# Sliding-window attention in zero-padded blocks of 128 keys, and carried memories' rows loaded straight into 128-row tiles

## The chip, the cores and the metric

One Trainium2 chip, one of its cores. A core has five engines with instruction queues of their own: TensorE (PE in the profile, with its weight loads as PEld), VectorE (DVE), ScalarE (ACT), GpSimd (POOL) and SyncE (SP, which here only starts DMAs). The metric is the device time of one launch in microseconds (us), the median of several runs.

## The reference

Two layers of a trunk, applied to a prompt of 512 tokens without history and to 8 samples of 16 tokens with carried state; width 1024, all in fp32. Per layer:

```
u = rms_norm(x);  z = u @ w_in                       # 1024 -> 10504 columns, split into 14 pieces
y_a = (rg_lru(conv(xa)) * gelu(ga)) @ w_oa           # linear recurrence
y_b = (rms_norm(mlstm(q,k,v,gates)) * sigmoid(mo)) @ w_ob     # 4 heads of 256, matrix memories C
y_c = banded_attention(q,k,v, window 128, sinks) @ w_oc       # 16 heads of 64, 2 key/value heads
x += (sigmoid(g_a)*y_a + sigmoid(g_b)*y_b + sigmoid(g_c)*y_c) @ w_out
x += square(relu(rms_norm(x) @ w_up)) @ w_down       # 1024 -> 4096 -> 1024
```

Attention works on chunks of 64 queries. A chunk sees the 128 keys before it and its own 64, so 192 keys; the first two chunks of the prompt see 64 and 128. A sample's 16 queries see 128 cached keys and 16 new ones. Scores get a softmax with an extra sink term in the denominator, `p = exp(s-mx) / (sum + exp(sink-mx))`, and then `p @ v`. For the samples the mLSTM also updates each carried memory, `C_new = decay*C + sum_s wk_s k_s v_s^T`, for 8 samples x 4 heads.

## The kernel before

Tokens are 640 columns (512 of the prompt, 128 of the samples). Every large projection is `gemm_w` (line 154: weights stationary, 320 token columns a matmul, issued on line 167) or `gemm_x` (line 173: tokens stationary, 256 weight columns, line 185). For accuracy a weight block is split into a rounded part (ACT, line 142) and a remainder (DVE, line 143), and both are multiplied in fp32r, which the trace shows as one instruction a matmul; a plain fp32 matmul is two, a transpose (a matmul against the identity) one.

The program is written with a scheduler that fixes each engine's order at build time from its own cost estimates. So attention and mLSTM matmuls stand among those of projections, and an engine runs its list strictly in order. What follows is the code around the change.

Attention (`attention`, from line 603). For each of 8 pairs of query heads, `prompt_pair` (line 694) goes through four groups G of two 64-query chunks. A group has one PSUM bank from `ps_small` (four such banks). Scores (line 705) are [128 = two heads x 64 queries, up to 192 keys] a chunk; `softmax` (line 679) takes the maximum, the exponentials, the sums and the division; the result P is transposed in two pieces, 128 keys (line 714) and 64 keys (line 717); both are copied to SBUF (pT), and line 740 multiplies them with the values: a matmul whose contraction has 128 rows and one with 64. Odd chunks need values that are shifted by 64 rows, which the copy vB holds. `sample_group` (line 748) does the same for one key/value head's 8 samples, two at a time, with 128 cached keys (line 786) and 16 new ones (line 787, contraction of 16 rows). It runs twice a layer, after the second and the fourth block of query heads; after the second run attention is over.

mLSTM (`mlstm`, from line 402). For each head, `sample` (line 425) writes the split keys and values of the samples to a DRAM scratch (sdr) and reads them back by groups of two samples: `rows(g)` loads 48 rows (16 of each of three products) into a staging tile `kvr`, of which there are two, DVE copies that into the fp32r tile `kvs` (line 441), of which there is one, and line 461 multiplies with a contraction of 48 rows. Line 457 reads the memory with the queries, line 463 adds the product to it.

Of the kernel before, what the change touches and what calls it, by code (L numbers as in the profile page):

```python
# [60 lines left out]
def trunk(ctx: ExitStack, tc: tile.TileContext, I, O):  # L61
# [3 lines left out]
    pe, act, dve, pool, sp = nc.tensor, nc.scalar, nc.vector, nc.gpsimd, nc.sync  # L65
# [11 lines left out]
    ident = cs[:, 0:128]  # L77
# [16 lines left out]
    def ps_small():  # L94
        return psB.tile([128, 512], F32, name="psb", tag="psb")
# [184 lines left out]
    with tc.tile_pool(name="ld", bufs=1) as ld:  # L280
# [121 lines left out]
    def mlstm(l, gp, gpp, mp, half, hdp):  # L402
# [200 lines left out]
    def attention(l, ap):  # L603
# [16 lines left out]
        def norm_rope(q, n, tabs, out):  # L620
# [6 lines left out]
            dve.tensor_tensor(t1, q, q, ALU.mult)  # L627
# [49 lines left out]

        def softmax(units, sink, P):

            n = len(units)  # L680
            sm = ap.tile([128, 20], F32, name="ssm", tag="ssm", bufs=3)
            mx, nm, sums, es, rc = [sm[:, 4 * i:4 * i + n] for i in range(5)]
            for i, (s, k) in enumerate(units):
                dve.tensor_reduce(mx[:, i:i + 1], s, AX.X, ALU.max)
            dve.tensor_scalar(nm, mx, sink, -1.0, op0=ALU.max, op1=ALU.mult)  # L685
            for i, (s, k) in enumerate(units):
                act.activation(P[:, i, 0:k], s, AF.Exp, bias=nm[:, i:i + 1], accum_out=sums[:, i:i + 1])  # L687
# [3 lines left out]
            for i, (s, k) in enumerate(units):  # L691
                dve.tensor_scalar(P[:, i, 0:k], P[:, i, 0:k], rc[:, i:i + 1], None, op0=ALU.mult)

        def prompt_pair(pair, g, q):
            yo = ap.tile([128, 512], F32, name="yo", tag="yo", bufs=2)
            for G in range(4):
                units = []
                ps = ps_small()
                for cc in range(2):
                    c = 2 * G + cc  # L700
                    k0 = max(0, 64 * (c - 2))
                    k = 64 * (c + 1) - k0
                    s = ps[:, 256 * cc:256 * cc + 192]
                    for part in range(2):
                        pe.matmul(s, q[:, c].rearrange("p a d -> p (a d)"), kh[g][:, part, k0:k0 + 192],  # L705
                                  start=(part == 0), stop=(part == 1))
                    units.append((s[:, 0:k], k))
                P = ap.tile([128, 2, 192], F32, name="P", tag="P", bufs=4)
                softmax(units, sinkp[:, pair:pair + 1], P)
                pT = ap.tile([128, 4, 128], F32, name="pT", tag="pT", bufs=2)  # L710
                for cc in range(2):
                    c = 2 * G + cc
                    if c > 0:
                        pe.transpose(ps[:, 128 * cc:128 * cc + 128], P[:, cc, 0:128], ident)  # L714
                    if c != 1:
                        o = 0 if c == 0 else 128
                        pe.transpose(ps[0:64, 256 + 128 * cc:384 + 128 * cc], P[:, cc, o:o + 64], ident)
                pv = ps.rearrange("p (a b) -> p a b", a=4)
                if G == 0:
                    act.copy(pT[:, 1, :], pv[:, 1, :])  # L720
                    dve.tensor_copy(pT[0:64, 2, :], pv[0:64, 2, :])
                else:
                    act.copy(pT[:, 0:2, :], pv[:, 0:2, :])
                    dve.tensor_copy(pT[0:64, 2:4, :], pv[0:64, 2:4, :])
                for cc in range(2):
                    c = 2 * G + cc
                    o = ps[:, 128 * cc:128 * cc + 128]

                    def vv_(t_, j, n):
                        return t_[0:n, j, g].rearrange("p a d -> p (a d)")  # L730
                    if c == 1:
                        parts = [(vv_(vd, 0, 128), pT[:, 1, :])]
                    elif c == 0:
                        parts = [(vv_(vd, 0, 64), pT[0:64, 2, :])]
                    elif c % 2 == 0:
                        parts = [(vv_(vd, (c - 2) // 2, 128), pT[:, 0, :]), (vv_(vd, c // 2, 64), pT[0:64, 2, :])]
                    else:
                        parts = [(vv_(vB, (c - 3) // 2, 128), pT[:, 1, :]), (vv_(vB, (c - 1) // 2, 64), pT[0:64, 3, :])]
                    for n, (a, b) in enumerate(parts):
                        pe.matmul(o, a, b, start=(n == 0), stop=(n == len(parts) - 1))  # L740
                pov = ps[:, 0:256].rearrange("p (c r q) -> p c r q", c=2, r=2)
                for r in range(2):
                    sl = slice(64 * r, 64 * r + 64)
                    eng = act.copy if r else dve.tensor_copy
                    eng(yo[sl, 128 * G:128 * G + 128].rearrange("p (c q) -> p c q", c=2), pov[sl, :, r, :])  # L745
            sp.dma_start(ydr[1][128 * pair:128 * pair + 128, 0:512], yo)

        def sample_group(g):
            vn = ap.tile([16, 8, 2, 64], F32, name="vn", tag="t2")
            for b in range(DB):  # L750
                sp.dma_start(vn[:, b], vd[16 * b:16 * b + 16, 4, g])
# [12 lines left out]
            act.copy(kcT[:, :, 128:144], ks[g].rearrange("p (b s) -> p b s", s=16))  # L764
            yo = ap.tile([128, 4, 128], F32, name="yo", tag="yo", bufs=2)
            for b2 in range(4):
                units = []
                ps = ps_small()
                for bb in range(2):
                    s = ps[:, 256 * bb:256 * bb + 144]  # L770
                    b = 2 * b2 + bb
                    pe.matmul(s, qsm[:, b].rearrange("p a q -> p (a q)"), kcT[:, b, :], start=True, stop=True)
                    units.append((s, 144))
                P = ap.tile([128, 2, 192], F32, name="P", tag="P", bufs=4)
                softmax(units, sinks[:, g:g + 1], P)
                pT = ap.tile([128, 4, 128], F32, name="pT", tag="pT", bufs=2)
                for bb in range(2):
                    pe.transpose(ps[:, 128 * bb:128 * bb + 128], P[:, bb, 0:128], ident)
                    pe.transpose(ps[0:16, 256 + 128 * bb:384 + 128 * bb], P[:, bb, 128:144], ident)
                pv = ps.rearrange("p (a b) -> p a b", a=4)  # L780
                act.copy(pT[:, 0:2, :], pv[:, 0:2, :])
                dve.tensor_copy(pT[0:16, 2:4, :], pv[0:16, 2:4, :])
                for bb in range(2):
                    b = 2 * b2 + bb
                    o = ps[:, 128 * bb:128 * bb + 128]
                    pe.matmul(o, vc[:, b].rearrange("p a d -> p (a d)"), pT[:, bb, :], start=True, stop=False)  # L786
                    pe.matmul(o, vn[:, b].rearrange("p a d -> p (a d)"), pT[0:16, 2 + bb, :], start=False, stop=True)  # L787
                pov = ps[:, 0:256].rearrange("p (b i r q) -> p b i r q", b=2, i=4, r=2)
                for r in range(2):
                    sl = slice(64 * r, 64 * r + 64)  # L790
                    eng = act.copy if r else dve.tensor_copy
                    eng(yo[sl, :, 32 * b2:32 * b2 + 32].rearrange("p i (b q) -> p b i q", b=2), pov[sl, :, :, r, :])
# [422 lines left out]
```

## Time and profile before

| | us |
|---|---|
| median of 3 runs (lowest to highest) | 3022.73 (3021.82 to 3025.65) |
| the profiled execution | 3022.11 |
| its span, first to last instruction | 3020.3 |
| PE busy | 2980.8 (99%) |
| DVE busy | 1594.3 (53%) |
| ACT busy | 1162.2 (38%) |
| POOL busy | 295.5 (10%) |

Matmuls are pipelined: the one that follows starts while the one before drains, so the mean duration of a group of matmuls is longer than what it adds to the time. What one adds is the distance between the starts, or the ends, of neighbours. Times in the timeline count from the span's start; the first layer ends at about 1520 us, the second repeats it. Attention's first scores stand at 250 us and its last products at 514 us, mLSTM's samples between 590 and 880 us.

### The profile page before, as it was taken

Reading aid. Unit: us, or ns where it says so; the run is one execution under the profiler, and the core shown is the slowest. Engines: PE = TensorE matmul, PEld = TensorE weight load, DVE = VectorE, ACT = ScalarE, POOL = GpSimd, SP = SyncE. Lnnn points to the kernel's source line nnn. Section 1 sums busy time; section 2 is a strip of 40 time slices with the busy share of each in tenths; the row PEclk is TensorE's granted clock in tenths of the full one; section 3 lists DMA queues with packets and bytes.
Section 4 is the critical chain, followed back from the end, with each engine's and each line's share of the span. In section 5 each row is a group of like instructions: output and inputs, shape, how many; then the busy total and the mean of one; then the engine's idle time right before and its main releaser. Section 6 shows DMA issues by size and latency. Waiting matters only on the chain.

```text
span 3020.3 us, 51634 instructions
## 1 busy us (share of the span) xinstructions
PE 2980.8 (99%) x20742; PEld 2894.7 (96%) x20742; DVE 1594.3 (53%) x3460; ACT 1162.2 (38%) x2409; POOL 295.5 (10%) x357
## 2 busy tenths in 40 slices
PE   8999999999999999999999999999999999999999
PEld 8999998999999999999999999989999999999999
DVE  7967565445564443333479666554455544433332
ACT  5754443433432332232348443433333323322322
POOL 0300000111102010010012000001010120100100
PEclk9999998999999999999999999989999999999999
DMA  5232221444565322222322322224444743222222
GB/s 167 71 110 76 66 89 58 133 131 139 152 214 180 105 70 84 71 72 83 101 85 66 114 81 66 90 73 132 133 145 147 243 123 111 70 76 79 70 79 76
DMA packets 291216, 319.59 MB, mean 106 GB/s; under 512 B 26424, under 2 KB 259688, under 8 KB 290944
## 3 DMA queue, kind: packets, MB, share of 16 engines
q1 hardware_dynamic: 281440, 300.03, 32.6%
q10 hardware_dynamic: 9536, 16.26, 1.5%
q8 instruction: 163, 2.67, 0.4%
q14 instruction: 77, 0.63, 0.1%
HBM read 255.76 MB, written 62.04 MB: 105 GB/s over the span
## 4 chain that ended last, share of the span: by engine, by line
PE 92%; DVE 3%; DMA 2%; ACT 2%; issue 1%; SPq 0%; POOL 0%; ACTq 0%; DVEq 0%; POOLq 0%
PE acc L167 62%; PE acc L185 17%; PE psb L740 3%; PE psb L461 1%; PE psb L705 1%; PE psb L457 1%; PE psb L550 1%; PE psb L997 1%; DVE wlo L143 1%; PE psb L546 1%; PE psb L787 1%; PE psb L536 1%; PE psb L543 1%; PE psb L786 0%; PE psb L714 0%
## 5 line engine op out<-in xcount | busy, mean ns | idle before, releaser
L167 PE MATMUL acc<-at,whi 128*128 128x320 f32 x8960 | 1394.4, 311 | 4.2 <-DVE sg L904 2.4
L167 PEld LDWEIGHTS acc<-at,whi 128*128 128x128 f32 x8960 | 1331.8, 188 | 11.5 <-DVE sg L904 3.0
L167 PE MATMUL acc<-at,wlo 128*128 128x320 f32 x4480 | 721.4, 310 | 0.0
L167 PEld LDWEIGHTS acc<-at,wlo 128*128 128x128 f32 x4480 | 670.0, 188 | 3.4
L142 ACT CAST whi<-wraw 128x512 fp32r<-128x512 f32 (+1 forms) x712 | 428.5, 619 | 596.1 <-PE acc L167 524.5
L143 DVE TENSOR_TENSOR wlo<-wraw,whi 128x512 fp32r<-128x512 f32 (+1 forms) x712 | 474.1, 704 | 294.7 <-ACT whi L142 191.7
L185 PE MATMUL acc<-whi,at 128*128 128x256 f32 (+1 forms) x3040 | 411.9, 286 | 10.1 <-DVE sg L864 3.0
L185 PEld LDWEIGHTS acc<-whi,at 128*128 128x128 f32 x3040 | 380.6, 190 | 15.7 <-ACT vt L497 3.9
L185 PE MATMUL acc<-wlo,at 128*128 128x256 f32 (+1 forms) x1520 | 219.1, 284 | 0.0
L185 PEld LDWEIGHTS acc<-wlo,at 128*128 128x128 f32 x1520 | 196.7, 190 | 1.3
L1136 POOL TENSOR_TENSOR ha<-ha 128x640 f32<-128x640 f32 x64 | 82.2, 1284 | 824.3 <-DVE ha L1135 824.3
L1144 DVE TENSOR_TENSOR x<-x,acc 128x640 f32<-128x640 f32 x56 | 45.8, 818 | 153.4 <-PE acc L167 153.4
L116 DVE TENSOR_TENSOR at<-ha,at 128x640 fp32r<-128x640 f32 x64 | 52.8, 825 | 135.3 <-ACT at L115 135.3
L1134 ACT ACTIVATE ha<-acc 128x640 f32<-128x640 f32 x64 | 45.2, 706 | 188.6 <-PE acc L167 188.6
L1135 DVE TENSOR_TENSOR ha<-ha,rbc 128x640 f32<-128x640 f32 x64 | 52.8, 826 | 109.6 <-ACT ha L1134 109.6
L687 ACT ACTIVATE P<-psb,ssm 128x192 f32<-128x192 f32 (+3 forms) x160 | 62.2, 397 | 59.1 <-DVE ssm L685 55.6
L115 ACT CAST at<-ha 128x640 fp32r<-128x640 f32 x64 | 46.6, 728 | 75.1 <-POOL ha L1136 74.3
L453 ACT CAST ch<-cb 128x516 fp32r<-128x516 f32 x64 | 39.4, 625 | 92.7 <-PE psb L457 54.9
L865 ACT ACTIVATE sg<-sg,cvh 128x640 f32<-128x640 f32 x48 | 39.9, 831 | 77.7 <-DVE sg L864 77.7
L463 DVE SCALAR_TENSOR_TENSOR cb<-cb,decb,psb 128x258 f32<-128x258 f32 x128 | 57.2, 478 | 19.7 <-PE psb L461 19.3
L481 POOL TENSOR_SCALAR mo<-mo 128x256 f32<-128x256 f32 x40 | 38.0, 953 | 262.0 <-ACT mo L480 262.0
L745 DVE COPY yo<-psb 64x128 f32<-64x128 f32 x64 | 18.1, 283 | 82.7 <-PE psb L740 82.5
(336 smaller groups left out, 2797.8 us busy)
## 6 DMA issues: line engine op xcount, KB each, us to landing
wraw<-in_w_in SPq DMA_DIRECT2D x160, 512.0 KB
wraw<-in_w_up SPq DMA_DIRECT2D x64, 512.0 KB
wraw<-in_w_down SPq DMA_DIRECT2D x64, 512.0 KB
cb<-in_state_mlstm_C SPq DMA_DIRECT2D x64, 256.0 KB
out_C_s<-cb SPq DMA_DIRECT2D x64, 256.0 KB
gdr<-sg ACTq DMA_DIRECT2D x32, 320.0 KB
rl<-ydr SPq DMA_DIRECT2D x32, 320.0 KB
sg<-gdr SPq DMA_DIRECT2D x32, 320.0 KB
```

The costliest lines, as they stand in the source:

```text
L115: act.copy(dst[:, 0], src)
L116: dve.tensor_tensor(dst[:, 1], src, dst[:, 0].bitcast(F32), ALU.subtract)
L142: act.copy(hi[:, :, :n], r)
L143: dve.tensor_tensor(lo[:, :, :n], r, hi[:, :, :n].bitcast(F32), ALU.subtract)
L167: pe.matmul(acc[:, s, 0:320], lhs, xs[k][:, part, 320 * s:320 * s + 320], start=(i == 0 and k == 0 and part == 0), stop=(i == 1 and k == 7),)
L185: pe.matmul(o, xs[k][:, part, 128 * t:128 * t + 128], wt[:, k % KQ, 0:n], start=(i == 0 and k == 0 and part == 0), stop=(i == 1 and k == 7),)
L463: dve.scalar_tensor_tensor(cb[:, kt, :], cb[:, kt, :], decb[:, h, 4 + b:5 + b], ps[:, 0:258], op0=ALU.mult, op1=ALU.add)
L687: act.activation(P[:, i, 0:k], s, AF.Exp, bias=nm[:, i:i + 1], accum_out=sums[:, i:i + 1])
L740: pe.matmul(o, a, b, start=(n == 0), stop=(n == len(parts) - 1))
L1135: dve.tensor_tensor(a, a, rbc, ALU.mult)
L1136: pool.tensor_tensor(a, a, a, ALU.mult)
L1144: dve.tensor_tensor(halves(xs[k]), halves(xs[k]), acc[:, :, 0:320], ALU.add)
```

## The change

In the prompt, scores are computed for as many keys as a chunk has, and the probabilities go into one of four tiles `prob` that were set to zero once a layer. In it each chunk has 256 columns, two blocks of 128 keys that both chunks of a group share, and it writes its 64, 128 or 192 probabilities at their place. So a group has four transposes of 128x128 (two for the first group), one copy of the bank to SBUF, and then one matmul a block for both chunks: contraction 128, 256 columns. vB and its copies go. One `softmax` now serves two groups (four chunks): the maxima and the divisions of two chunks are one instruction each, the division being a tensor_tensor with a broadcast factor. The samples are done four at a time in the same way: the new keys' values `vn` get 128 rows, 112 of them zero, and `sprob` (4 x 256 columns) is set to zero once a group.

In mLSTM the staging tile and its copy go: `rows(g)` loads the 48 rows straight into one of two `kvs` tiles of 128 rows, zero elsewhere, and the matmul contracts over 128 rows. `st` gets a buffer of its own. In `norm_rope` a square moves from DVE to ACT.

```diff
 def mlstm(...):
+        kvs = [mp.tile([128, 2, 514], F32R, name=f"kvs{g}") for g in range(2)]
+        for t_ in kvs:
+            pool.memset(t_.bitcast(F32), 0.0)
...
-            st = mp.tile([128, 1028], F32R, name="st", tag="kvr", bufs=2)
+            st = mp.tile([128, 1028], F32R, name="st", tag="st", bufs=1)
...
             def rows(g):
-                raw = mp.tile([48, 2, 514], F32, name="kvr", tag="kvr", bufs=2)
+                kv = kvs[g % 2]
                 sd = sdr[h][32 * g:32 * g + 32].rearrange("(b s) i d -> s i b d", s=16)
                 for i in range(3):
-                    sp.dma_start(raw[16 * i:16 * i + 16], sd[:, i])
-                kv = mp.tile([48, 2, 514], F32R, name="kvs", tag="kvs", bufs=1)
-                dve.tensor_copy(kv, raw)
+                    sp.dma_start(kv[16 * i:16 * i + 16].bitcast(F32), sd[:, i])
                 return kv
...
 def attention(l, ap):
-            dve.tensor_tensor(t1, q, q, ALU.mult)
+            act.activation(t1, q, AF.Square)
...
-        vB = ap.tile([128, 4, 2, 2, 64], F32, name="vB")
-        act.copy(vB[0:64], vd[64:128, 0:4])
-        act.copy(vB[64:128, 0:3], vd[0:64, 1:4])
+        probs = [ap.tile([128, 640], F32, name=f"prob{i}") for i in range(4)]
+        for t_ in probs:
+            pool.memset(t_, 0.0)
...
-        def softmax(units, sink, P):
+        def softmax(maxima, exps, norms, sink):
-            for i, (s, k) in enumerate(units):
-                dve.tensor_reduce(mx[:, i:i + 1], s, AX.X, ALU.max)
+            for i, n, s in maxima:
+                dve.tensor_reduce(mx[:, i:i + n], s, AX.X, ALU.max)
...
-            for i, (s, k) in enumerate(units):
-                dve.tensor_scalar(P[:, i, 0:k], P[:, i, 0:k], rc[:, i:i + 1], None, op0=ALU.mult)
+            for i, n, v in norms:
+                dve.tensor_tensor(v, v, rc[:, i:i + n].unsqueeze(2).to_broadcast(list(v.shape)), ALU.mult)
...
         def prompt_pair(pair, g, q):
-            for G in range(4):
+            for H in range(2):
+                for i in range(2):
+                    G = 2 * H + i
...
+                        s = ps[:, 256 * cc:256 * cc + k]
+                        o = 256 * cc + (64 * cc if G else 128)
+                        exps.append((2 * i + cc, s, P[:, o:o + k]))
...
+                softmax(maxima, exps, norms, sinkp[:, pair:pair + 1])
...
+                    for kb in range(lo // 256, 2):
+                        for cc in range(2):
+                            o = 256 * kb + 128 * cc
+                            pe.transpose(ps[:, o:o + 128], P[:, 256 * cc + 128 * kb:256 * cc + 128 * kb + 128], ident)
+                    (dve.tensor_copy if i else act.copy)(pT[:, lo:512], ps[:, lo:512])
...
+                    for kb in range(0 if G else 1, 2):
+                        pe.matmul(po[:, 256 * i:256 * i + 256], vd[:, G - 1 + kb, g].rearrange("p a d -> p (a d)"),
+                                  pTs[i][:, 256 * kb:256 * kb + 256], start=(kb == 0 or G == 0), stop=(kb == 1))
...
         def sample_group(g):
-            vn = ap.tile([16, 8, 2, 64], F32, name="vn", tag="t2")
+            vn = ap.tile([128, 8, 2, 64], F32, name="vn", tag="t2")
+            pool.memset(vn, 0.0)
...
+            sprob = ap.tile([128, 4, 256], F32, name="sprob", tag="t1")
+            pool.memset(sprob, 0.0)
```

In the new file the lines after the first edit move: scores 713, the prompt's transposes 735 and value products 743, the samples' scores 781, transposes 793 and value products 803, the memories' update product 463.

PE's list in the first layer, in the fourth pair of query heads (P and prob are probabilities, pT their transposes, psb a PSUM bank, vd and vB values). Before:

```order
L740 MATMUL psb<-pT,vd 128x128 x2
L185 MATMUL acc<-wlo,at 128x256
L714 MATMUL psb<-cs,P 128x128
L717 MATMUL psb<-cs,P 64x128
L714 MATMUL psb<-cs,P 128x128
L717 MATMUL psb<-cs,P 64x128
L185 MATMUL acc<-wlo,at 128x256
L740 MATMUL psb<-pT,vd 128x128 x2
L740 MATMUL psb<-pT,vB 128x128 x2
```

and after:

```order
L743 MATMUL psb<-pT,vd 128x256
L185 MATMUL acc<-wlo,at 128x256 x2
L735 MATMUL psb<-cs,prob_2370 128x128 x4
L735 MATMUL psb<-cs,prob_2371 128x128 x4
L185 MATMUL acc<-whi,at 128x256 x2
L743 MATMUL psb<-pT,vd 128x256 x2
L767 MATMUL psb<-cs,kc 128x128 x4
L185 MATMUL acc<-whi,at 128x256 x11
L743 MATMUL psb<-pT,vd 128x256 x4
```

The output shape that stands here hides the contraction: in the first list each `x2` of line 740 is one product over 128 rows and one over 64 (the very first group has one of each), in the second every product is over 128 rows. The transposes keep their number, the value products halve in number and double in width.

PE's list at the end of attention in the first layer (kcT holds the cached keys, qsm the samples' queries). Before:

```order
L740 MATMUL psb<-pT,vB 128x128 x2
L772 MATMUL psb<-kcT,qsm 128x144 x8
L778 MATMUL psb<-cs,P 128x128
L779 MATMUL psb<-cs,P 16x128
L778 MATMUL psb<-cs,P 128x128
```

After:

```order
L781 MATMUL psb<-kcT,qsm 128x144 x4
L167 MATMUL acc<-at,wlo 128x320 x2
L185 MATMUL acc<-whi,at 128x256 x16
L185 MATMUL acc<-wlo,at 128x256 x8
L185 MATMUL acc<-whi,at 128x256 x16
L185 MATMUL acc<-wlo,at 128x256 x2
L793 MATMUL psb<-cs,sprob 128x128 x8
```

Before, the samples' transposes stand right behind their scores; after, 42 matmuls of mLSTM's first projection and 2 of another stand between them. Those 42 stood behind the sample group before.

SP's list in mLSTM's first head, where the third group of rows is loaded (cb is a carried memory, wraw a raw weight block). Before:

```order
L439 DMA kvr<-sdr_80 16x2x514 [waits DMAHW3_49,DMAHW4_49,DMAHW2_49,DVE_49]
L439 DMA kvr<-sdr_80 16x2x514 x2
L566 DMA out_C_p<-cp 128x2x256 [waits DVE_49]
L511 DMA dmat<-adr 128x640 [waits DVE_49]
L465 DMA out_C_s<-cb 128x2x256 [waits DMAHW5_49,DVE_49]
```

After:

```order
L467 DMA out_C_s<-cb 128x2x256 [waits DMAHW2_49,DVE_49]
L451 DMA cb<-in_state_mlstm_C 128x2x256 [waits DMAHW3_49,DMAHW2_49,Pool_49]
L443 DMA kvs_5412<-sdr_80 16x2x514 [waits DMAHW4_49,PE_49]
L443 DMA kvs_5412<-sdr_80 16x2x514 [waits DMAHW5_49]
L467 DMA out_C_s<-cb 128x2x256 [waits DMAHW6_49,DVE_49]
```

The load waited for DVE's copy of the first group; it now waits for PE's products with the first group, and stands behind the first memory's store and the sixth memory's load.

## Rows read from the trace of the kernel before

**Rows 1.** The page, busy time by engine: us, share of the span, instructions.

```profile
PE 2980.8 (99%) x20742; PEld 2894.7 (96%) x20742; DVE 1594.3 (53%) x3460; ACT 1162.2 (38%) x2409; POOL 295.5 (10%) x357
```

**Rows 2.** The page, the chain that ended last, shares of the span by engine.

```profile
PE 92%; DVE 3%; DMA 2%; ACT 2%; issue 1%; SPq 0%; POOL 0%; ACTq 0%; DVEq 0%; POOLq 0%
```

**Rows 3.** PE's groups by line and shape: count, busy us, mean ns, idle before.

```profile
L461 PE MATMUL psb<-kvs 48*128 48x258 f32 x128 | 37.9, 348 | 2.4 <-DVE kvs L441 1.8 <-DVE csum L472 0.5
L740 PE MATMUL psb<-pT,vd 64*128 64x128 f32 x128 | 31.1, 322 | 0.5 <-DVE pT L721 0.5
...
L740 PE MATMUL psb<-pT,vd 128*128 128x128 f32 x128 | 26.3, 293 | 0.0
...
L740 PE MATMUL psb<-pT,vB 128*128 128x128 f32 x96 | 23.4, 326 | 0.0
L740 PE MATMUL psb<-pT,vB 64*128 64x128 f32 x96 | 23.3, 322 | 0.0
...
L787 PE MATMUL psb<-pT,vn 16*128 16x128 f32 x64 | 20.4, 409 | 0.0
```

**Rows 4.** PE's timeline, value products: start, duration (us); a row shows its first shape.

```profile
485.51 0.27 PE L717 MATMUL psb<-cs,P 128*64 128x128 f32 x1
485.62 0.80 PE L740 MATMUL psb<-pT,vd 128*128 128x128 f32 x4
486.35 0.90 PE L740 MATMUL psb<-pT,vB 128*128 128x128 f32 x4
487.19 0.33 PE L762 MATMUL psb<-cs,kc 128*128 128x128 f32 x1
```

**Rows 5.** PE's timeline in mLSTM's samples.

```profile
591.82 0.29 PE L457 MATMUL psb<-ch,qm 128*128 128x258 f32 x1
591.94 0.28 PE L457 MATMUL psb<-cl,qm 128*128 128x258 f32 x1
592.15 0.50 PE L461 MATMUL psb<-kvs 48*128 48x258 f32 x2
592.58 0.39 PE L457 MATMUL psb<-ch,qm 128*128 128x258 f32 x1
592.80 0.28 PE L457 MATMUL psb<-cl,qm 128*128 128x258 f32 x1
```

**Rows 6.** PE's timeline, fp32 products of 128 rows and 257 columns.

```profile
585.29 1.03 PE L546 MATMUL psb<-cp,qs 128*128 128x257 f32 x4
586.16 1.03 PE L550 MATMUL psb<-vt,kw 128*128 128x257 f32 x4
```

**Rows 7.** Stretch after the last samples' scores: PE, PEld, DVE, ACT, POOL busy, PEclk, DMA.

```profile
493.50:520.00 26.50, 21.04 (x85) 16.37 (x85) 12.10 (x48) 7.71 (x33) 2.97 (x5) 0.61 0.04 11
```

**Rows 8.** Waits of PE: us in total, times, longest.

```profile
PE psb L778 <- DVE ssm L689: 7.1, 2, 3.6
...
PE psb L461 <- DVE kvs L441: 1.8, 3, 1.4
```

**Rows 9.** Timeline at the end of attention.

```profile
491.30 2.23 PE L772 MATMUL psb<-kcT,qsm 128*128 128x144 f32 x16
...
494.73 2.25 DVE L692 TENSOR_SCALAR P<-P,ssm 128x144 f32<-128x144 f32 x2
...
494.78 2.02 POOL L412 MEMSET qm<- 128x2304 f32 x1
```

**Rows 10.** Timeline of one pair's softmax, from its last scores to its first transpose.

```profile
475.81 1.05 PE L705 MATMUL psb<-kh,qp 128*128 128x192 f32 x8
...
482.42 0.27 PE L717 MATMUL psb<-cs,P 128*64 128x128 f32 x1
```

**Rows 11.** The chain in order of time, projections: start, us, count.

```profile
390.60 14.09 PE acc L167 x96
...
544.96 5.68 PE acc L185 x48
```

**Rows 12.** Waits of DVE's copy of the rows: us, times.

```profile
  DMA kvr<-sdr: 18.3, 7
```

More of the change, by code (lines that the diff above doesn't have):

```diff
@@ new lines, in prompt_pair @@
+            for H in range(2):
+                pss, Ps, maxima, exps, norms = [], [], [], [], []
+                for i in range(2):
+                    G = 2 * H + i
+                    ps = ps_small()
+                    P = probs[turn[0] % 4]
+                    turn[0] += 1
+                    for cc in range(2):
+                        c = 2 * G + cc
+                        k0 = max(0, 64 * (c - 2))
+                        k = 64 * (c + 1) - k0
+                        s = ps[:, 256 * cc:256 * cc + k]
+                        for part in range(2):
+                            pe.matmul(s, q[:, c].rearrange("p a d -> p (a d)"), kh[g][:, part, k0:k0 + k],
+                                      start=(part == 0), stop=(part == 1))
+                        o = 256 * cc + (64 * cc if G else 128)
+                        exps.append((2 * i + cc, s, P[:, o:o + k]))
+                        if G == 0:
+                            maxima.append((2 * i + cc, 1, s))
+                    if G:
+                        maxima.append((2 * i, 2, ps.rearrange("p (c k) -> p c k", c=2)[:, :, 0:192]))
+                        norms.append((2 * i, 2, P.rearrange("p (c k) -> p c k", c=2)[:, :, 0:192]))
+                    else:
+                        norms.append((2 * i, 2, P[:, 0:512].rearrange("p (c k) -> p c k", c=2)[:, :, 128:256]))
+                    pss.append(ps)
+                    Ps.append(P)
+                softmax(maxima, exps, norms, sinkp[:, pair:pair + 1])
+                pTs = []
+                for i in range(2):
+                    G = 2 * H + i
+                    ps, P = pss[i], Ps[i]
+                    lo = 0 if G else 256
+                    for kb in range(lo // 256, 2):
+                        for cc in range(2):
+                            o = 256 * kb + 128 * cc
+                            pe.transpose(ps[:, o:o + 128], P[:, 256 * cc + 128 * kb:256 * cc + 128 * kb + 128], ident)
+                    pT = ap.tile([128, 512], F32, name="pT", tag="pT", bufs=3)
+                    (dve.tensor_copy if i else act.copy)(pT[:, lo:512], ps[:, lo:512])
+                    pTs.append(pT)
+                po = pss[0]
+                for i in range(2):
+                    G = 2 * H + i
+                    for kb in range(0 if G else 1, 2):
+                        pe.matmul(po[:, 256 * i:256 * i + 256], vd[:, G - 1 + kb, g].rearrange("p a d -> p (a d)"),
+                                  pTs[i][:, 256 * kb:256 * kb + 256], start=(kb == 0 or G == 0), stop=(kb == 1))
+                pov = po.rearrange("p (c r q) -> p c r q", c=4, r=2)
@@ L764, in sample_group @@
             act.copy(kcT[:, :, 128:144], ks[g].rearrange("p (b s) -> p b s", s=16))
+            sprob = ap.tile([128, 4, 256], F32, name="sprob", tag="t1")
+            pool.memset(sprob, 0.0)
             yo = ap.tile([128, 4, 128], F32, name="yo", tag="yo", bufs=2)
[L766 to L788, printed above, removed]
@@ new lines, in sample_group @@
+            for b4 in range(2):
+                pss, maxima, exps, norms = [], [], [], []
+                for i in range(2):
+                    ps = ps_small()
+                    P = sprob[:, 2 * i:2 * i + 2]
+                    for bb in range(2):
+                        s = ps[:, 256 * bb:256 * bb + 144]
+                        b = 4 * b4 + 2 * i + bb
+                        pe.matmul(s, qsm[:, b].rearrange("p a q -> p (a q)"), kcT[:, b, :], start=True, stop=True)
+                        exps.append((2 * i + bb, s, P[:, bb, 0:144]))
+                    maxima.append((2 * i, 2, ps.rearrange("p (c k) -> p c k", c=2)[:, :, 0:144]))
+                    norms.append((2 * i, 2, P[:, :, 0:144]))
+                    pss.append(ps)
+                softmax(maxima, exps, norms, sinks[:, g:g + 1])
+                pTs = []
+                for i in range(2):
+                    ps = pss[i]
+                    for bb in range(2):
+                        for kb in range(2):
+                            o = 256 * bb + 128 * kb
+                            pe.transpose(ps[:, o:o + 128], sprob[:, 2 * i + bb, 128 * kb:128 * kb + 128], ident)
+                    pT = ap.tile([128, 512], F32, name="pT", tag="pT", bufs=3)
+                    (dve.tensor_copy if i else act.copy)(pT, ps)
+                    pTs.append(pT)
+                po = pss[0]
+                for i in range(2):
+                    for bb in range(2):
+                        b = 4 * b4 + 2 * i + bb
+                        o = po[:, 256 * i + 128 * bb:256 * i + 128 * bb + 128]
+                        for kb, t_ in enumerate((vc, vn)):
+                            pe.matmul(o, t_[:, b].rearrange("p a d -> p (a d)"),
+                                      pTs[i][:, 256 * bb + 128 * kb:256 * bb + 128 * kb + 128], start=(kb == 0), stop=(kb == 1))
+                pov = po.rearrange("p (b i r q) -> p b i r q", b=4, i=4, r=2)
@@ L791, in sample_group @@
                     eng = act.copy if r else dve.tensor_copy
[L792 removed]
+                    eng(yo[sl, :, 64 * b4:64 * b4 + 64].rearrange("p i (b q) -> p b i q", b=4), pov[sl, :, :, r, :])
             sp.dma_start(ydr[1][512 * g:512 * g + 512, 512:640].rearrange("(i p) q -> p i q", p=128), yo)
```

55 lines of the change are left out of this document (6 added, 49 removed).

## The prediction

> **What bounds the kernel now.** I read the page first: PE is busy for 2980.8 of 3020.3 us, DVE for 53% and ACT for 38% [rows 1], and the chain that ended last is PE for 92% of its length [rows 2]. So a change is worth what it takes off PE's list or adds to it, and what PE waits for; work of DVE, ACT, POOL and the DMA queues is paid only where PE stands still for it. Busy says nothing of how well PE is used, though, so the next view is PE's groups by shape [rows 3]. Their means (293 to 409 ns) are latencies of pipelined matmuls; the reader is to see that some contract over 64, 48 or 16 rows while everything around them contracts over 128. What such a matmul costs is seen in the timeline, from distances between neighbours.
>
> In [rows 4], the transpose that starts at 485.51 ends at 485.78 and is followed 0.11 us later by the first value product; four products run from 485.62 to 486.42, four more end at 487.25, and the next transpose at 487.52. The nine instructions moved the end by 1.74 us. At 0.11 each they would have moved it by 0.99. Among them the contraction changes four times (128 to 64 rows and back, twice), so a change costs 0.75/4 = 0.19 us. The same is seen of 48 rows [rows 5]: neighbours of 128 rows start 0.12 us apart, the two products of 48 rows move the end from 592.22 to 592.65, the next of 128 rows to 592.97: 0.75 us for three that should need 0.36, so 0.195 for each of two changes. The second of two products of 48 rows costs nothing extra, so it is the change that is dear, not the small contraction.
>
> Last, PE's waits are few. The largest that the change touches is at the end of attention, where the samples' transposes wait for their softmax, 3.6 us a layer [rows 8], and the 26.5 us after the last samples' scores ran at a mean granted clock of 0.61 [rows 7] (the second layer has the same stretch): between the levels 2.4 and 1.2 GHz that is some 78% of it, 20.7 us, at the lower one. It fell right after PE's wait.
>
> **The change, part by part.**
>
> Contraction always 128. Number of changes that go: in the prompt a pair has one product of 64 rows in its first group (in and out: 2) and two in each of three others (4 each), so 14, and 16 pairs in two layers make 224. Samples: 32 products of 16 rows, 64 changes. Memories: 128 products of 48 rows [rows 3], which by PE's list stand in 86 runs of one or two: 172. Together 460 x 0.19 = 87.4 us, all on PE's path. What replaces them contracts over 128 rows, so nothing else pays.
>
> Value products. Before, 224 in the prompt, two instructions each (448 in rows 3), at 0.11: 49.3 us without the changes. After, 112 of 256 columns, 224 instructions; fp32 products of 257 columns start 0.87 us apart by fours [rows 6], 0.217 each: 48.6 us. That is -0.7. The transposes keep their number, 288, and 0.11 us. A quarter of the scores get narrower, but scores of 192 columns are already 0.11 apart (eight take 1.05 us with a last latency of 0.28) [rows 10], as are transposes of 128 [rows 4]: nothing.
>
> End of attention. The stretch of [rows 7] holds 85 instructions, 9.6 us at 0.11 (0.118 for the 31 projections [rows 11]), and 16 changes already counted, 3.0 us. So 26.5 - 9.6 - 3.0 = 13.9 us a layer are wait and lower clock. In the new list the first four samples' scores are followed by 15 matmuls of line 167 (0.147 each [rows 11]), the other four's scores (1.0 us) and 42 of line 185 (0.118): 8.2 us of work before the first transpose. The old softmax began by 492.1 and was ready at 497.04, when its first transpose started, the division slowed to 2.25 us for two [rows 9]: 5 us. So the wait should go and with it the reason for the lower clock. Bounds 0 and -27.8 for two layers; I take 13 of 13.9, -26, nearer to the full cover that the list shows.
>
> Softmax over two groups. The first transpose now waits for four exponentials, not two. It came 6.6 us after its scores began [rows 10] and did not wait, with projections between. The new list has 43 or more projections there in most pairs, 6.3 us, and 47 of line 185, 5.5 us, in one. Bounds 0 and 16 pairs x 1 us; I take +3.
>
> Carried rows. DVE's 32 copies go, and with them PE's wait of 1.8 us for them [rows 8]. But the load into a kvs tile now waits for PE's products of two groups earlier, not for a copy: on SP the memories' stores and loads are queued behind it, and PE waits for those. DVE's copy had to wait for seven loads, 2.6 us each [rows 12]. Sixteen loads are bound in this way (third and fourth group of each head, two layers): bounds -1.8 and 16 x 2.6 = +42. By PE's list some 11 us of its own work lie between the release and the next use, so I take -1.
>
> New memsets on POOL. 2304 columns took 2.02 us [rows 9], so the new 8712 columns a layer are 7.6 us. In rows 9 DVE's two divisions stretched to 2.25 us beside such a memset. Bounds 0 and +15 for both layers if DVE stood still for each and PE for DVE; I take 0, since PE has projections at those places. The Trainium skill (SBUF — State Buffer, "Who interferes with whom") says that DVE's tensor_scalar can take the port pair it shares with GpSimd, while a tensor_tensor with two SBUF inputs contends only with a GpSimd instruction that reads SBUF. The stretched tensor_scalar agrees with that; by it the new division, a tensor_tensor, would not be held up by a memset at all, which would leave the 0.
>
> The square on ACT, the wider copies and the merged maxima are off PE's path: DVE and ACT have half their time free [rows 1]. If that cover failed, it would be as late probabilities, which the +3 holds.
>
> Sum against the profiled execution: 3022.1 - 87.4 - 0.7 - 26 + 3 - 1 = 2910. The median of the runs is 0.6 us above that execution, so 2911.
>
> **Rivals.**
>
> The end of attention stays as it is: softmax for four samples is a longer chain, PE waits again, the clock falls again. For it: nothing in the trace shows the new order at work. Against: 8.2 us of cover for a chain of 5. Then 2911 + 26 = 2937. Chance 14%.
>
> New waits in mLSTM or at the pairs' transposes: half of the 42 us, or the 13 left of the softmax's 16. 2925 to 2955. Chance 13%.
>
> More goes: waits of projections for their copies, spread over attention and mLSTM, shrink as DVE and ACT get less work: 2885 to 2897. Chance 10%.
>
> Padding is worth nothing. If the 0.19 us came from where the small products stand in the dependences (a wait that the profile doesn't name) and not from their rows, they stay: 3022.1 - 0.7 = about 3021. Against it, rows 4 and 5: the idle before those groups is small [rows 3] and the price is equal at 64 and 48 rows. Chance 4%. The Trainium skill (TensorE: Matmul & The Clock Gate, table "Why this matters for your kernels") has such a rule, a single matmul over 32 rows takes the same time as one over 128; for the second of a run the rows agree. The Trainium skill (TensorEngine Tiling (Array Packing), "Key Properties") also says, against it, that changing the tiling mode drains TensorE; the 0.19 us bear that out.
>
> Slower: the softmax of two groups leaves PE dry. If at each of 16 pairs the four-chunk chain ran to the 6.6 us of rows 10 beyond its cover, and the second half's transposes came 2 to 3 us later still, PE would lose 9 us a pair, 144 in all: 2908 + 144 = 3052, before any loss of clock. It decides from 7 us a pair. Against: it needs the chain to double, while two groups were already in flight at once before. Chance 3%.
>
> **How the numbers follow.** The forecast, 2898 to 2924, has 56%. The range of 8 in 10 takes in the first rival and most of the second and third: 2888 to 2945. A measurement can tell 0.2%, 6 us, from no change. Faster by more than that are all cases but the last two, and a little of the second's tail: 95%. Within it lies most of the padding rival: 2.5%. Slower: 2.5%.
>
> **What would show it.** In the new profile the value products (line 743) stand 0.22 us apart with no step at their first or last, the update products (463) 0.12 from their neighbours, and PE's groups have no shape of 64, 48 or 16 rows. PE's first sample transposes (793) have no wait above 1 us, and the stretch behind them has a granted clock near 1. Attention (200 to 520 us) is shorter by about 39 us, mLSTM's samples by 17 a layer. I am wrong if line 743 or 463 keep steps of 0.19, if PE waits for `sprob` or `kvs`, or if the clock still falls at attention's end.

## The result and the profile after

| | before | after |
|---|---|---|
| median of 4 runs each, same chip (us) | 3022.28 (3020.36 to 3025.65) | 2926.13 (2925.10 to 2928.09) |
| the profiled execution / its span | 3022.11 / 3020.3 | 2926.99 / 2925.1 |

The ratio is 0.9678, with a 95% interval of 0.9667 to 0.9690: 96 us faster, where 111 were forecast (2911). The time lies 2 us above the forecast's 2898 to 2924 and inside the wider range of 2888 to 2945. The page of after, busy time by engine and the chain that ended last, answering to [rows 1, 2]:

```profile
PE 2881.9 (99%) x20518; PEld 2849.7 (97%) x20518; DVE 1539.6 (53%) x3074; ACT 1144.9 (39%) x2295; POOL 304.2 (10%) x377
...
PE 90%; DVE 4%; DMA 3%; ACT 2%; issue 1%; SPq 0%; POOL 0%; DVEq 0%; ACTq 0%; POOLq 0%
PE acc L167 63%; PE acc L185 16%; DMA out_C_s<-cb 2%; PE psb L743 2%; PE psb L713 1%; PE psb L552 1%; PE psb L735 1%; PE psb L1014 1%; PE psb L548 1%; DVE wlo L143 1%; DMA cb<-in_state_mlstm_C 1%; PE psb L459 1%; PE psb L538 1%; PE psb L545 1%; PE psb L803 0%
```

PE is still the bound, 99 us less busy. The memories' transfers, `out_C_s<-cb` and `cb<-in_state_mlstm_C`, take 71 us of the chain; before they took 16. That is the first sign of where the missing 15 us are.

PE's groups by shape (count | busy us, mean ns | idle before), answering to [rows 3]:

```profile
L743 PE MATMUL psb<-pT,vd 128*128 128x256 f32 x224 | 58.0, 380 | 0.0
L463 PE MATMUL psb<-kvs 128*128 128x258 f32 x128 | 36.5, 296 | 4.7 <-DVE cb L465 3.5 <-DVE csum L474 0.8
...
L803 PE MATMUL psb<-pT,vn 128*128 128x128 f32 x64 | 12.4, 275 | 0.0
```

Each of these groups now contracts over 128 rows. Two stretches of PE's timeline (start, duration), value products and an update product, answering to [rows 4, 5]:

```profile
453.28 1.03 PE L743 MATMUL psb<-pT,vd 128*128 128x256 f32 x4
453.96 1.08 PE L167 MATMUL acc<-at,whi 128*128 128x320 f32 x5
454.88 1.02 PE L743 MATMUL psb<-pT,vd 128*128 128x256 f32 x4
455.74 0.60 PE L767 MATMUL psb<-cs,kc 128*128 128x128 f32 x4
```
```profile
549.88 0.28 PE L459 MATMUL psb<-cl,qm 128*128 128x258 f32 x1
550.00 0.40 PE L463 MATMUL psb<-kvs 128*128 128x258 f32 x2
550.24 0.28 PE L459 MATMUL psb<-ch,qm 128*128 128x258 f32 x1
```

The ends say it: the second four value products move the end from 455.04 to 455.90, 0.215 each, and the four transposes behind them by 0.44, 0.11 each. The update products move it by 0.12 each, the next by 0.12. No step at either border.

The end of attention, answering to [rows 7 to 9]: PE's timeline with its waits, and the two windows that hold it and what follows (columns as in [rows 7]).

```profile
463.76 2.04 PE L185 MATMUL acc<-whi,at 128*128 128x256 f32 x16
465.63 0.39 PE L185 MATMUL acc<-wlo,at 128*128 128x256 f32 x2
465.87 1.03 PE L793 MATMUL psb<-cs,sprob 128*128 128x128 f32 x8
...
474.81 1.45 PE L185 MATMUL acc<-whi,at 128*128 128x256 f32 x10 [1.72 <-ACT ktok L487]
```
```profile
464.00:474.00 10.00, 8.87 (x77) 8.29 (x75) 4.45 (x12) 3.49 (x13) 0.96 (x1) 1.00 0.41 124
474.00:520.00 46.00, 45.19 (x352) 44.50 (x353) 28.43 (x83) 19.53 (x47) 0.00 (x0) 1.00 0.43 121
```

The transposes (L793) stand behind projections without a wait, and the granted clock is 1.00. A wait of 1.72 us for `ktok` is left; before, PE waited 1.41 us for it inside the slow stretch (2.8 us in both layers).

PE's waits, us, times, longest, answering to [rows 8]:

```profile
PE psb L587 <- DVE num L581: 5.2, 3, 3.6
PE acc L185 <- ACT vt L499: 4.5, 7, 2.0
...
PE psb L463 <- DVE cb L465: 3.5, 5, 1.1
...
PE psb L459 <- ACT ch L455: 2.6, 4, 1.0
```

All four are mLSTM's. To sum such things I took, for each of PE's instructions, the distance of its end from the one before, less the pace of its kind (the median of the fastest quarter of its line and shape). What is left over is a step, where the contraction changes its rows, or else a wait, slow clock or small excess. Each row is the one profiled execution; those of kvs3 (2940.5 us) and ml_pad_staged (3014.6) were the longest of their kernels, 7 and 6 us above the median. In us, both layers together, attention up to its last product and mLSTM from there to its last transpose:

```
                  median   attention       mLSTM
                           steps  other    steps  other
before            3022.3    60.2   29.7     43.0   18.1
after             2926.1     0     16.7      1.2   46.5
att_only          2939.5     0     16.7     39.9   19.5
ml_only           2999.7    58.8   29.3      5.0   43.7
ml_pad_staged     3008.8    60.2   28.4      5.0   50.1
kvs48             2942.6     0     16.7     47.3   17.0
grouped           3001.4    42.6   27.0     43.4   19.1
samples2          2919.4     0     16.4      1.2   36.8
kvs3              2933.0     0     16.7      1.2   56.6
cb7               2903.3     0     16.7      1.2   24.1
before_cb7        3012.7    57.7   21.8     44.5   15.3
samp_only         2991.3    42.8   20.9     41.0   19.4
cb7_s2            2902.4     0     16.4      1.2   20.8
cb7_s2_pool       2896.5     0     16.3      1.2   15.4
```

So after gained 102 us of steps and 13 of attention's other losses, and gave 28 back in mLSTM. Two entries stand in unlike columns and cancel in the 28: the waits for `ktok`, which before fall on a change of rows and count as steps (3.75 us) and in after count as mLSTM's (4.0), and 4.0 us of lower clock behind attention, which before stand under mLSTM. The experiments, named in the table, ask whether the steps hang on the rows, what gave the 28 back, and what ended the slow clock.

### The profile page after: what moved, and what is told of

It reads as the page before. It is cut to its first block, busy times and chain, and to the rows that moved or that the text cites. A ratio compares the mean times of both kernels' runs of the same rounds, so it can differ in the third digit from the quotient of the medians.

```text
span 2925.1 us, 50762 instructions
## 1 busy us (share of the span) xinstructions
PE 2881.9 (99%) x20518; PEld 2849.7 (97%) x20518; DVE 1539.6 (53%) x3074; ACT 1144.9 (39%) x2295; POOL 304.2 (10%) x377
## 4 chain that ended last, share of the span: by engine, by line
PE 90%; DVE 4%; DMA 3%; ACT 2%; issue 1%; SPq 0%; POOL 0%; DVEq 0%; ACTq 0%; POOLq 0%
PE acc L167 63%; PE acc L185 16%; DMA out_C_s<-cb 2%; PE psb L743 2%; PE psb L713 1%; PE psb L552 1%; PE psb L735 1%; PE psb L1014 1%; PE psb L548 1%; DVE wlo L143 1%; DMA cb<-in_state_mlstm_C 1%; PE psb L459 1%; PE psb L538 1%; PE psb L545 1%; PE psb L803 0%
## 5 line engine op out<-in xcount | busy, mean ns | idle before, releaser
L691 ACT ACTIVATE prob<-psb,ssm 128x192 f32<-128x192 f32 (+2 forms) x128 | 49.6, 406 | 39.9 <-DVE ssm L689 39.9
L456 DVE TENSOR_TENSOR cl<-cb,ch 128x516 fp32r<-128x516 f32 x64 | 43.8, 694 | 29.5 <-ACT ch L455 29.4
```

Source lines behind the costliest of these rows:

```text
L691: act.activation(o, s, AF.Exp, bias=nm[:, i:i + 1], accum_out=sums[:, i:i + 1])
```

## The experiments

Medians are of 4 runs or more; every kernel ran against before on its chip (3020.5 to 3021.2 us).

**The price of a change of rows.** `grouped`, the kernel before with the second chunk's two products in reverse order:

```diff
+                    if cc == 1:
+                        parts = parts[::-1]
                     for n, (a, b) in enumerate(parts):
```

> The kernel before with one edit: of the two chunks of a group in the prompt's attention the second multiplies its 64-row part first and its 128-row part after, so the rows go 128, 64, 64, 128 instead of 128, 64, 128, 64. Same products, same rows, same sizes; three groups of each pair lose 2 of 4 changes, 96 in all. If the 0.2 us hang on the change of rows: 96 x 0.2 = 19 less, about 3002. If they hang on the small product itself, or on its place in the dependences: 3021.

Measured: 3001.37, ratio 0.9935 (0.9920 to 0.9949). Its timeline, one group of products between transposes:

```profile
476.49 0.27 PE L717 MATMUL psb<-cs,P 128*64 128x128 f32 x1
476.60 0.80 PE L742 MATMUL psb<-pT,vd 128*128 128x128 f32 x4
477.24 0.80 PE L742 MATMUL psb<-pT,vB 64*128 64x128 f32 x4
477.88 0.60 PE L764 MATMUL psb<-cs,kc 128*128 128x128 f32 x4
```

From 476.76 to 478.04 the eight instructions move the end by 1.28, against 1.47 for the same eight in [rows 4], and the way back to 128 rows is no longer paid twice. Nothing was padded and as many small products are left; the time fell by 19.2 us for 96 changes, 0.20 each. The rival that padding is worth nothing has fallen: it is the change that costs.

**The halves.** `att_only` and `ml_only` are before with the new `attention` alone and the new `mlstm` alone; `ml_pad_staged` is before with this edit only:

```diff
+        kvs = mp.tile([128, 2, 514], F32R, name="kvs")
+        pool.memset(kvs.bitcast(F32), 0.0)
...
-                kv = mp.tile([48, 2, 514], F32R, name="kvs", tag="kvs", bufs=1)
-                dve.tensor_copy(kv, raw)
+                kv = kvs
+                dve.tensor_copy(kv[0:48], raw)
```

and `kvs48` is after with

```diff
-        kvs = [mp.tile([128, 2, 514], F32R, name=f"kvs{g}") for g in range(2)]
-        for t_ in kvs:
-            pool.memset(t_.bitcast(F32), 0.0)
+        kvs = [mp.tile([48, 2, 514], F32R, name=f"kvs{g}") for g in range(2)]
```

> The kernel before with the new attention alone. If the two halves add up, attention's share of the 96 us is what the traces show there: 97.9 us of steps, waits and slow clock on PE before against 23.7 after, so 74 less, about 2947 us. If the new waits of mLSTM (27 us more than before) came from attention's edit, because it shifts the rest of PE's list, they would appear here too: about 2970.

> The kernel before with the new mLSTM alone. 172 changes of contraction go, 39 us in the trace of before. If mLSTM's own edit brings the new waits of 27 us, 3022 - 39 + 27, and a few us less for two waits that go behind mLSTM: about 3006 to 3010. If the waits need both halves together: about 2984.

> The kernel before with one edit: DVE's copy writes its 48 rows into a 128-row tile that was set to zero once a layer, so the products contract over 128 rows; staging tiles, copies and loads stay. Theory A (the load into kvs that waits for PE's products holds up the memories' transfers behind it on SP): no such wait here, so the 39 us go and no new waits come, about 2984. Theory B (mLSTM's samples are bound by the memories' way through five buffers, store, load, split, as soon as PE gets faster, whatever the load path is): the waits come here too, 3005 or more.

> The kernel after with kvs tiles of 48 rows: loads as after, without staging, but contraction over 48 rows again. The 172 changes come back, 39 us. Theory A: the waits stay beside them, about 2965. Theory B: PE's slower products hide most of the 27 us of waits again, about 2940 to 2945. That small products cost nothing by their rows (padding is worth nothing): 2926.

Measured: 2939.52 (ratio 0.9727, 0.9710 to 0.9743), 2999.68 (0.9926, 0.9908 to 0.9944), 3008.76 (0.9961, 0.9946 to 0.9975) and 2942.61 (0.9738, 0.9723 to 0.9752). The first two came out 7 and 6 us below the nearer of their numbers, which is not explained; the other two as theory B has it. The halves nearly add up: 81.6 + 21.5 = 103, against 96. Attention alone brings no new waits to mLSTM (19.5). Theory A falls: with staging and copy kept, padding brings the waits all the same (50.1), and with the new loads but 48 rows they are gone (17.0; in that order of PE's list 230 changes came back, not 172, 47.3 us of steps). They come with PE's speed and not with the load path, as theory B says. That the direct loads are worth something shows only beside padding: ml_only is 9.1 us faster than ml_pad_staged, where PE still waits 4.6 us for DVE's copy of the rows and 10 of the 50.1 us are lower clock.

**What PE then waits for.** In after's second layer, ACT's timeline, SP's issues and PE's:

```profile
2102.04 0.62 ACT L455 CAST ch<-cb 128x516 fp32r<-128x516 f32 x1 [2.25 <-DMA cb<-in_state_mlstm_C]
2108.63 0.62 ACT L455 CAST ch<-cb 128x516 fp32r<-128x516 f32 x1 [5.97 <-DMA cb<-in_state_mlstm_C]
2109.28 0.47 ACT L499 ACTIVATE vt<-acc,rtok 128x256 f32<-128x256 f32 x1
```
```profile
2100.94 0.43 SPq L467 DMA_DIRECT2D out_C_s<-cb  x1
...
2103.51 0.37 SPq L451 DMA_DIRECT2D cb<-in_state_mlstm_C  x1
```
```profile
2109.80 1.33 PE L185 MATMUL acc<-whi,at 128*128 128x256 f32 x9 [1.97 <-ACT vt L499]
```

A memory's load goes out at 2103.51; SP's loads wait for the stores of the memories five places earlier (105.0 us in 51 waits in all; before it was 92.0 in 49, with less of it passed on to PE). ACT stands 5.97 us before the split of that memory, and `vt`, the copy of a projection's finished product out of PSUM, which has nothing to do with memories, stands behind it in ACT's list. PE, which needs the accumulator that `vt` frees, waits 1.97 us. DVE has the same: behind four columns that must be copied into the next buffer stands the norm that ends in `num`.

```profile
2195.65 0.17 DVE L452 COPY cb<-nT 128x4 f32<-128x4 f32 x1 [2.91 <-DMA out_C_s<-cb]
...
2199.47 0.17 DVE L452 COPY cb<-nT 128x4 f32<-128x4 f32 x1 [1.58 <-DMA out_C_s<-cb]
2199.55 2.06 DVE L581 SCALAR_TENSOR_TENSOR num<-num,fin,mo 128x256 f32<-128x256 f32 x5
```

PE waited 3.6 us for that `num`, the longest of the waits above. So the buffers were the next thing to try. `kvs3` is after with three kvs tiles in turn, `cb7` with seven memory buffers; both let two small tiles share other tiles' places for room. `before_cb7` is before with the edit of `cb7`.

```diff
-                kv = kvs[g % 2]
+                kv = kvs[(4 * h + g) % 3]
```
```diff
-                cb = mp.tile([128, 2, 258], F32, name="cb", tag="cb", bufs=5)
+                cb = mp.tile([128, 2, 258], F32, name="cb", tag="cb", bufs=7)
```

> The kernel after with three kvs tiles in turn, so a load waits for products three groups back, not two. Theory A for what is left: some of the waits go, 5 to 15 us, 2911 to 2921. Theory B (either): 2922 to 2930.

> The kernel after with seven buffers for the memories instead of five (two small tiles share the place of others to make room). Theory B1 (a memory's load waits for the store of the one five places earlier, and the split and all that is behind it on ACT and DVE waits for the load): the new waits of mLSTM, 28 us over both layers, go for the most part, about 2900 to 2911. Theory B2 (the waits come from the order of ACT's and DVE's own work, not from buffers): 2922 to 2930. Theory A has fallen as the main cause, since the waits came without the load path too.

> The kernel before with seven buffers for the memories instead of five, nothing else. Theory B1 as the reason for the shortfall: before, the changes of contraction kept PE slow enough that five buffers nearly did; all its waits and small excesses in mLSTM are 18 us over both layers, of which a part stays with seven buffers too (after: 24 us with seven), so 0 to 6 less, 3015 to 3022. If seven buffers simply are worth 23 us in any version, the shortfall is not a waits-for-padding exchange: about 2998.

Measured: kvs3 2933.01 (0.9711, 0.9692 to 0.9729), cb7 2903.31 (0.9608, 0.9593 to 0.9622), before_cb7 3012.66 (0.9976, 0.9966 to 0.9986). How long engines stood idle ahead of instructions that use `cb`, and for what, in us and times, in before:

```profile
  DMA cb<-in_state_mlstm_C: 29.3, 14
...
  ACT ch L453: 8.7, 11
```

in after:

```profile
  DMA cb<-in_state_mlstm_C: 64.0, 26
...
  ACT ch L455: 29.4, 25
```

and in cb7, where no wait for the load is left (DVE's small copies into the buffers still wait for stores):

```profile
  DMA out_C_s<-cb: 47.3, 28
...
  ACT ch L455: 3.0, 7
```

Seven buffers take 22 of after's 46.5 us, which is B1; kvs3, with the same sharing of small tiles, gains nothing. They do next to nothing for before's mLSTM (steps and other together 59.8 for 61.1). before_cb7 came out 2 us below the 3015 to 3022 of B1; the 8 us that it gains are attention's, where the rearranged list of the second layer no longer has the wait of [rows 8]. So before, five buffers were enough for PE because the steps left the memories time. A third kvs tile does not help; that it costs 7 us, with more waits for `vt` and `ch` in a differently ordered list, is not explained.

**The end of attention.** `samples2` is after with the samples' attention two at a time; `samp_only` is before with just that padded sample part. The core of both:

```diff
-            for b4 in range(2):
+            for b2 in range(4):
...
-                    P = sprob[:, 2 * i:2 * i + 2]
+                P = sprob[:, 2 * (b2 % 2):2 * (b2 % 2) + 2]
```

> The kernel after with the samples' attention two at a time, as before, still padded to 128 rows: four softmaxes a group instead of two. My step says that the wait of 3.6 us at the end of attention went because the list puts 8 us of other matmuls between scores and transposes of four samples; with two at a time the list may put the transposes right behind the scores again, and then wait and slow clock come back, up to 26 us, about 2950. If the padding itself or the division's new form took them away: 2926.

> The kernel before with the samples' attention alone padded to 128 rows, two samples a softmax; the prompt's attention and mLSTM as before. 64 changes of contraction go, of which 32 ran at the lower clock: in the trace of before 14.9 us for these and 6.4 for the others, 21. In PE's list the last group's transposes stand right behind their scores, as before, in the first layer at least. My step (the wait goes because other matmuls stand in between): the wait of 3.5 us and the slow clock behind it stay, about 3001. Rival (the sparse 16-row products brought the clock down, padding alone ends it): 20 us more, about 2981.

Measured: samples2 2919.38 (0.9664, 0.9648 to 0.9680), samp_only 2991.31 (0.9906, 0.9890 to 0.9921). In samples2 PE's list puts 40 projections between scores and transposes here too, and no wait for the softmax comes back; doing four samples at once is not what brought the cover. The time, lower than both numbers, has its 7 us less in mLSTM's losses (36.8). samp_only fits neither number. (Its 21 us for the changes of rows had counted the waits for `ktok` among them, 3.75 us; PE still waits for it.) Its first layer has no projection in between, and yet:

```profile
486.13 2.23 PE L790 MATMUL psb<-kcT,qsm 128*128 128x144 f32 x16
490.24 0.63 PE L798 MATMUL psb<-cs,sprob 128*128 128x128 f32 x4 [1.89 <-DVE ssm L758]
491.83 0.63 PE L798 MATMUL psb<-cs,sprob 128*128 128x128 f32 x4 [0.96 <-DVE sprob L761]
```
```profile
490.00:494.00 4.00, 2.79 (x22) 2.53 (x23) 3.32 (x13) 2.59 (x13) 1.81 (x2) 1.00 0.00 0
494.00:498.00 4.00, 3.73 (x33) 3.33 (x31) 1.89 (x7) 1.36 (x4) 0.00 (x0) 1.00 0.03 6
```

The waits are 1.89 and 0.96 us, not 3.6, and the clock stays at 1.00. (In the second layer, behind 1.89 and 1.04 us, it was at the lower level for 3.4 us.) Cover is one way to keep the clock up, then, not the only one. What kept it, the shorter waits or the missing changes behind them? Two traces have the one without the other, both in the second layer. In `grouped` the 16-row products are those of before, and the waits are nearly as short as in samp_only (PE's timeline, then a window with PE busy, PEclk and DMA):

```profile
1970.50 0.30 PE L780 MATMUL psb<-cs,P 128*128 128x128 f32 x1 [1.76 <-DVE P L692]
...
1972.66 0.30 PE L780 MATMUL psb<-cs,P 128*128 128x128 f32 x1 [1.53 <-DVE ssm L689]
```
```profile
1975.00:1980.00 5.00, 5.00 (x18) 0.50 0.00 0
```

The clock fell all the same and stayed low for some 20 us, as before. In `before_cb7` the 16-row products are those of before too, but 40 projections stand between the last scores and the transposes, and PE waits for none of them:

```profile
1990.00:1995.00 5.00, 5.00 (x41) 1.00 0.36 119
1995.00:2000.00 5.00, 5.00 (x29) 1.00 0.00 0
```

There, with the 16-row products between 1993.7 and 2000.4 us, the clock stays at 1.00 over the changes. (It was low for 6.8 us behind them, where PE waits 3.8 us for `ktok`.) So in these traces the 20 us of lower clock took both, waits and changes behind them; with either missing the clock was low for 3.4 us or not at all. Each is one layer of one execution, and grouped's two waits together are 0.4 us longer than samp_only's.

**A faster version.** `cb7_s2` joins cb7 and samples2; `cb7_s2_pool` also issues the memories' stores from POOL:

```diff
-                sp.dma_start(O["C_s"][l, b, h].rearrange("(k p) e -> p k e", p=128), cb[:, :, 0:256])
+                pool.dma_start(O["C_s"][l, b, h].rearrange("(k p) e -> p k e", p=128), cb[:, :, 0:256])
```

> The kernel after with seven buffers for the memories and the samples' attention two at a time. If the 7 us of the samples by twos came from mLSTM's waits, which seven buffers have taken already: 2900 to 2904. If they are a gain of attention's own: about 2896.

> The same with the memories' stores issued by POOL instead of SP, behind POOL's small copy that waits for the same DVE work anyway. SP stood 50 us in these issues' waits, with weights' and memories' loads behind them. If that made loads late: 5 to 10 us less than the run without, 2890 to 2898. If not, no difference.

Measured: 2902.43 (0.9611, 0.9594 to 0.9628) and 2896.54 (0.9590, 0.9575 to 0.9605). The gain of samples2 was the same waits that cb7 takes. The stores on POOL take 6 us more (its slowest run, 2897.13, is below the other's fastest, 2900.68) and bring mLSTM's other losses to 15.4. It beats before by 124 us and after by 30.

## Why the prediction was right, and where it was off

- **Changes of rows: right.** Of 472 changes 12 are left, so 460 went, as counted. The 428 at full clock were 87.1 us, 0.203 each; the 32 at attention's end ran at the lower clock and were 14.9 us, of which the sum had 6 here and the others under the next term. These 14.9 hold two waits for `ktok` (3.75 us with the changes that they fall on); the other 30 changes are 11.1 us beyond the pace at full clock, 0.37 each, and some 0.27 each beyond the 0.21 us that an instruction of 128 columns takes at the lower clock.
- **Value products: right.** 224 instructions at 0.218 make 48.9, against 48.6.
- **End of attention: right in size, its reason half shown.** 26 of 27.8 were forecast; waits, slow clock and surplus steps there were 28 us in before and 5.5 in after, so 23 went. What stays is the waits for `ktok` and `pT`, 3.9 us before and 3.8 after, which the forecast had among the 13.9 us a layer. That the list's cover is enough, after, samples2 and the second layer of before_cb7 show; samp_only shows that without the changes it was not needed.
- **Softmax over two groups: +3 forecast, 0 found.** PE's wait table has no transposes of the prompt (L735) in it.
- **Carried rows: the step that failed.** The forecast had -1 with bounds to +42, argued from the load that waits for PE: some 11 us of PE's own work were to cover it. mLSTM's other losses grew by 28 us. The mechanism is another one: the padded products let PE run ahead of the memories, whose five buffers were just enough for PE before; with seven, 22 of the 28 us go. "Nothing else pays", said of the products that contract over 128 rows, is the sentence that was wrong. The rival "new waits in mLSTM" had the place and 2925 to 2955 as its time, with half of the wrong bound as its price. The sum as it came out: steps and attention's other losses -115 (forecast with the softmax -110; the steps gave 6 more, at 0.203 for 0.19, the end of attention 3 less), paces of the instructions in the two stages -4 (forecast -1), mLSTM's other losses +28 (forecast -1), everything outside the two stages -5 (forecast 0): -95, the difference of the two spans.
- **Memsets on POOL: 0, right, with the cover that was named.** In after, beside a memset:

```profile
458.77 2.02 POOL L412 MEMSET qm<- 128x2304 f32 x1
458.99 1.96 DVE L689 TENSOR_SCALAR ssm<-ssm,sinks 128x4 f32<-128x4 f32 x1
459.12 1.83 DVE L143 TENSOR_TENSOR wlo<-wraw,whi 128x512 fp32r<-128x512 f32 x2
```
```profile
381.98 0.95 POOL L754 MEMSET vn<- 128x1024 f32 x1 [50.46 <-DVE ssm L693]
...
382.24 0.89 DVE L696 TENSOR_TENSOR prob<-prob,ssm 128x256 f32<-128x256 f32 x2
```

  A tensor_scalar of four columns, 0.23 us elsewhere, lasted as long as the memset, and the two tensor_tensors behind it in DVE's list ended with it; PE had projections and scores meanwhile. Two of the new divisions, tensor_tensor, lie beside the memset of `vn`: 0.89 us for the pair, as for such pairs elsewhere. That fits the Trainium skill (SBUF — State Buffer, "Who interferes with whom"): a tensor_scalar can lock the port that DVE shares with GpSimd, a tensor_tensor does not meet a memset there.
- **Attention and mLSTM by stage.** 38 and 36 us less in attention, as forecast (39); in mLSTM, from attention's last product to its own last transpose, 12 and 4 instead of 17.

## What to carry over

Count how often neighbours in PE's list change the rows of their contraction, not how many small products there are: padding with zeros, or only reversing a pair, takes the step away. Before booking the whole gain, ask what runs beside that stage on a fixed number of buffers: when PE gets faster there by 20 us a layer, a load that was just in time is late, and in-order lists pass that on to copies out of PSUM that have nothing to do with it. Buy the buffers together with the speed.

## What the runs showed of the hardware

A change between 128 and 64, 48 or 16 rows cost 0.20 us of PE's time at a granted clock of 1.00; at 0.5, between 128 and 16 rows, it cost some 0.27 us beyond the pace of that clock. The second of two alike cost nothing. The clock fell to 0.5 for some 20 us behind a wait of 3.5 us before, but after the wait of 3.6 us in after only for a few:

```profile
2200.00:2205.00 5.00, 4.65 (x20) 3.89 (x21) 4.35 (x10) 2.19 (x5) 0.00 (x0) 0.68 0.32 70
2205.00:2210.00 5.00, 5.00 (x44) 5.00 (x43) 1.89 (x3) 2.52 (x5) 0.85 (x1) 0.98 1.04 362
```

There PE had projections behind the wait; before, it had the samples' products with changes of rows between them. With those changes the clock stayed low for some 20 us behind waits of 1.76 and 1.53 us too (grouped), without them for 3.4 us or not at all behind 1.89 and 1.0 us (samp_only), and without a wait the changes left it at 1.00 (before_cb7).
